# A hybrid decoder layer on one core: attention in pairs of query blocks, input halves scaled one by one, and precedence for softmax and chain

## The chip, the cores and the metric

The kernel runs on one core of a Trainium2 chip. The time is device microseconds (us) of one execution. Each figure is the median of several executions unless it says that it is one profiled execution. The engines are TensorE (PE in the profile; PEld is its weight load), VectorE (DVE), ScalarE (ACT), GpSimd (POOL) and SyncE (SP), which issues the DMAs.

## The reference

The kernel computes one layer of a decoder with 1024 tokens and 1024 columns in float32:

```python
h = rmsnorm(x)                       # one combined input projection follows
# mixer A, 4 heads of 128: gated DeltaNet on q, k, v with a causal convolution of width 4,
#   S_t = a_t (I - b_t k_t k_t^T) S_{t-1} + b_t k_t v_t^T ;  o_t = S_t^T q_t
#   (in chunks: a triangular solve, then a chain of states), times silu(z)
# mixer B, 8 heads of 64: dilated sliding-window attention,
#   (window, dilation) in (128,1), (512,4), (2048,16), the branches merged
#   by their softmax denominators
x = x + concat(A, B) @ wo            # one output projection
gate, up = halves of causal_dwconv(rmsnorm(x) @ w_up)    # width 3
x = x + (silu(gate) * up) @ w_down                       # MLP of width 2816
out = rmsnorm(x)
```

The lines are shortened. Products of 128x128 weights with 512 tokens are written out as three products of high and low parts (`mm3`: xhi with whi, xlo with whi, xhi with wlo), so that the reduced-precision matmul mode gives nearly float32 results. Such a matmul is called a dense matmul below. Smaller products run in plain float32 as two or four passes.

## The kernel before, in words

The layer is one program in which many pieces of work are interleaved on TensorE.

*The planner.* `Weave` (lines 42 to 114) holds generator functions with levels: `norms` 0, `gates` 1, the preparation of keys 3, of queries and values 4, the chain 1, `attention` 5, `out_proj` 8, `dense` 9, the MLP 8. Each yields the time it has still to wait, by a model of each engine; `Weave.run` continues the ready one with the lowest level. The result is TensorE's written order. The other engines' orders come from the scheduler of the tile framework, which takes instructions by readiness and by their place in the program. Each engine then runs its own list strictly in order. All helper instructions of VectorE, ScalarE, GpSimd and SyncE are recorded at line 132, matmuls at line 177 and transposes at line 181.

*The stages in time.* From 0 to 107 us the first dense products and the preparation of keys run. From 107 to 229 the query and value columns run, with forward substitution and the merging of the inverse blocks in between. From 229 to 304 the four chains run: at each of 8 chunks of 128 tokens a state passes from TensorE to VectorE and ScalarE and back (`chain`, lines 733 to 797). From 313 to 493 attention runs, mixed with the dense products of the attention columns and of the gates z. Dense products and the output projection end at about 615; then come the second norm, the MLP's upper part (to 1028) and its lower part (to 1258). The MLP and its weights are not touched by the change.

*Dense columns.* `dense` (line 462) takes 25 columns of 128 one after the other (`first`, line 319, has done three columns of keys). A column has two halves of 512 tokens; each half is 24 dense matmuls into one bank of the `hf` ring. `scaled` then multiplies a half by the tokens' reciprocal norms (`rstdB`) on VectorE into a tile of 1024 (`xr`; `aqkv` for attention's columns, in the order of residue classes, which `apark` stores in DRAM). Key columns do that for each half when its bank is done; all others for both at the end of the column. `conv_silu` and `silu2` then work on the tile.

*Attention.* There are 4 pairs of heads (the two heads `e` of a pair lie in the two halves of the partitions) and 8 query blocks of 128 tokens for each, so 32 items. For an item, `scores` multiplies queries with up to 256 near keys and with keys of the same residue class, into two banks of tag `asc`; VectorE adds the mask and takes the extreme (`tensor_tensor_reduce`, in the profile CUSTOM_DVE_ANT), ScalarE takes the exponential with its sum, VectorE the reciprocal, and ScalarE multiplies by it. `turn` transposes the result through banks of tag `atr`: VectorE copies the near part to `pt` and ScalarE the far part to `pb`. `values` multiplies `pt` with the values into the bank `po`, and after four items `merge_classes` adds the far products and `give` copies `po` out to `oT`. `advance` orders it: scores of an item, values of the item two before, transposes of the item one before. `att_values` transposes the values of the next pair of heads between the last block of one and the first block of the next.

*Output projection.* `mixer_splits` loads each head's output `ot` (or takes `og` or `oT`), and splits it into `ohi` (ScalarE) and `olo` (VectorE). `out_proj` (line 1003) takes heads k = 0 to 7 in order, for two groups of output columns at once, once the last group of attention has begun.

Of the kernel before, what the change touches and what calls it, by code (L numbers as in the profile page):

```python
# [35 lines left out]
MSLACK = 1.5  # L36
MGAP = 0.6
# [79 lines left out]
class Engine:  # L117


    def __init__(self, wv, eng, name, fixed, per, lag=0.28):  # L120
        self.args = wv, eng, name, fixed, per, lag

    def __getattr__(self, op):
        wv, eng, name, fixed, per, lag = self.args

        def call(*a, **kw):
            aps = [x for x in a + tuple(kw.values()) if hasattr(x, "tensor")]
            acc = [kw["accum_out"]] if "accum_out" in kw else []
            n = float(np.prod(aps[0].shape[1:]))
            us = 0.3 + 0.165 * n if kw.get("op") == OP.pow else fixed + per * n  # L130
            wv.account(name, us, aps[:1] + acc, aps[1:], lag)
            return getattr(eng, op)(*a, **kw)  # L132
        return call


def hybrid_layer(tc, I, out):
# [3 lines left out]
    ac = Engine(wv, nc.scalar, "scalar", 0.12, 0.00085)  # L140
    po_ = Engine(wv, nc.gpsimd, "gpsimd", 0.15, 0.0021)
# [163 lines left out]
    wba = tile_(sp, [P, KT, 32], F32, "wba", "t1", 3)  # L305
# [117 lines left out]
    def conv_silu(pair, j, name, tag):  # L423
        xr = scaled(pair, "xr") if isinstance(pair, list) else pair
# [16 lines left out]
    def silu2(pair, name):  # L441
        xr = scaled(pair, "xr")
# [19 lines left out]
    def dense():  # L462
# [5 lines left out]
        for i, col in enumerate(DENSE):  # L468
# [7 lines left out]
            for hh in range(2):  # L476
                pt = bank("hf")
                yield wv.need(pt, *w)
                for k in range(KT):
                    mm3(pt, [t[:, k, :] for t in w], [t[:, half(hh)] for t in xs[k]], k == 0, k == KT - 1)  # L480
                    yield 0.0
                pair.append(pt)
                if kind == "k":
                    if hh == 0:
                        xr = A("xr", "go")
                    scaled(pair, "xr", t=xr, hs=(hh,))
# [3 lines left out]
            elif kind == "q":  # L490
                q = conv_silu(pair, h, "qT", "qa")
                wv.add(4, qprep(h, q))
            elif kind == "v":
                v = conv_silu(pair, 8 + h, "vT", "qa")
                wv.add(4, vprep(h, v))
            elif kind == "z":
                og = gated[h] = A("og", "kT*")
                sy.dma_start(og, mixer[h])
                ve.tensor_tensor(og, og, silu2(pair, "zz"), op=OP.mult)
            else:  # L500
                sy.dma_start(apark[h, col[2]], scaled(pair, "aqkv", True))
# [109 lines left out]
    def forward_sub():  # L611
# [6 lines left out]
        tmp = tile_(sp, [P, 256], F32, "tmp", "t1", 3)  # L618
# [111 lines left out]
    def chain(h):  # L730
# [14 lines left out]
        for c in range(NCH):  # L745
# [12 lines left out]
            else:  # L758
# [3 lines left out]
                ve.scalar_tensor_tensor(r, ps[:, 0:P], ngam[:, c, h:h + 1], vtok[:, cs], op0=OP.mult, op1=OP.add)  # L762
# [3 lines left out]
            if c < NCH - 1:  # L766
                wke = tile_(sp, [P, P], F32, "wke", "r" + tg, 1)
                ve.tensor_scalar(wke, ps[:, P:2 * P], ke[:, c:c + 1], None, op0=OP.mult)
            ac.activation(w, ps[:, P:2 * P], AF.Copy)
            if c < NCH - 1:  # L770
# [3 lines left out]
                if c == 0:  # L774
                    ve.tensor_copy(sn, ps[:, 2 * P:3 * P])
                else:
                    ve.scalar_tensor_tensor(sn, st, ge[:, c:c + 1], ps[:, 2 * P:3 * P], op0=OP.mult, op1=OP.add)
# [6 lines left out]
            ac.activation(vtok[:, cs], po[:, :P], AF.Copy, scale=rq[:, c:c + 1])  # L784
            if c:
                ve.scalar_tensor_tensor(vtok[:, cs], po[:, P:2 * P], gq[:, c:c + 1], vtok[:, cs], op0=OP.mult,
# [4 lines left out]
            ac.activation(osq, vtok[:, cs], AF.Square, accum_out=ms[:, c:c + 1])  # L791
# [30 lines left out]
    def att_values(vT):  # L822

        vn, vc = A("vn", "kt"), A("vc", "kt")
        for hh in range(2):
# [4 lines left out]
            ac.activation(vn[:, half(hh)], pt, AF.Copy)  # L830
        for c in range(4):
# [7 lines left out]
    def attention():  # L839
        for h in range(H):  # L840
            yield from wv.until(("o", h))
        mks = [A("mk", "go") for _ in range(2)]
        sy.dma_start(mks[0], I["mk"][0])
        sy.dma_start(mks[1], I["mk"][1])
        yield from wv.until(("a", 0, 2))
# [10 lines left out]
        def scores(it):  # L856
            n, q, k, nb = it["n"], it["q"], it["k"], it["nb"]
            pss = [bank("asc") for _ in range(2)]
            yield wv.need(*pss, q, k)
            k0 = max(n - 1, 0) * P  # L860
            n1_, n2_ = (n + 1) * P - k0, P * nb
            wd = n1_ + n2_
            for e, er in enumerate(HALVES):
                mm(pss[e][:, :n1_], q[er, n * P:(n + 1) * P], k[er, k0:k0 + n1_], 0.0009 * n1_)
            for c in range(4):
                o = slice(32 * c, 32 * c + 32)
                for e, er in enumerate(HALVES):
                    mm(pss[e][o, n1_:wd].rearrange("p (n u) -> p n u", u=32), q[er, n * P + 32 * c:n * P + 32 * c + 32],
                       by_block(k)[er, :4 * nb, c, :], 0.00025 * n2_, tile_position=(64 * e, 32 * c))
            sm = A("sm", "dv*", shape=(P, 2, 512))  # L870
            mx = tile_(sp, [P, 4], F32, "mx", "mx", 4)
            mn, den = mx[:, :2], mx[:, 2:]
            mv, m = mask(n)
            for e in range(2):
                ve.tensor_tensor_reduce(out=sm[:, e, :wd].rearrange("p (a b) -> p a b", a=m),
                                        in0=pss[e][:, :wd].rearrange("p (a b) -> p a b", a=m), in1=mv, scale=-0.125,
                                        scalar=-NEG, op0=OP.add, op1=OP.min, accum_out=mn[:, e:e + 1])
            for e in range(2):
                ac.activation(sm[:, e, :wd], sm[:, e, :wd], AF.Exp, bias=mn[:, e:e + 1], scale=-1.0,
                              accum_out=den[:, e:e + 1])  # L880

            ve.reciprocal(den, den)
            for e in range(2):
                ac.activation(sm[:, e, :wd], sm[:, e, :wd], AF.Copy, scale=den[:, e:e + 1])
            it.update(sm=sm, wd=wd, n1=n1_, k0=k0)

        def turn(it):
            sm, wd, n1_ = it["sm"], it["wd"], it["n1"]
            it["pt"] = []
            for e in range(2):  # L890
                pt = tile_(sp, [P, 256], F32, "pt", "t1", 3)
                it["pt"].append(pt)
                pp = bank("atr")
                yield wv.need(pp, sm)
                for i in range(wd // P):
                    tp(pp[:, i * P:(i + 1) * P], sm[:, e, i * P:(i + 1) * P])
                ve.tensor_copy(pt[:, :n1_], pp[:, :n1_])
                ac.activation(it["pb"][e][:, it["u"]].rearrange("p b t -> p (b t)"), pp[:, n1_:wd], AF.Copy)

        def values(it):  # L900
            u = it["u"]
            yield wv.need(it["po"], *it["pt"])
            for i in range(it["n1"] // P):
                for e, er in enumerate(HALVES):
                    mm(it["po"][er, u * P:(u + 1) * P], v8(it["vn"])[:, it["k0"] // P + i, er],
                       it["pt"][e][:, i * P:(i + 1) * P], 0.12, u == 0 and i == 0, False, skip_group_check=True)

        def merge_classes(g):
            vcv = g["vc"].rearrange("p (c b d) -> p c b d", c=4, b=2)
            po, nb = g["po"], g["nb"]  # L910
            yield wv.need(*g["pb"])
# [23 lines left out]
        def advance(it):  # L935
            if it is not None:
                yield from scores(it)
            pipe.insert(0, it)
            if len(pipe) > 2:
                done = pipe.pop()  # L940
                if done is not None:
                    yield from values(done)
                    if done["u"] == 3:
                        yield from merge_classes(done["g"])
                        give(done["g"])
            if len(pipe) > 1 and pipe[1] is not None:
                yield from turn(pipe[1])

        for pi in range(4):
            q, k, vn, vc = cur  # L950
            for hh in range(2):
# [9 lines left out]
                for u in range(4):  # L961
                    yield from advance(dict(n=4 * hh + u, u=u, q=q, k=k, vn=vn, nb=nb, po=po, pb=pb, g=g))
            if pi < 3:
                cur = qkv[:2] + (yield from att_values(qkv[2]))
        for _ in range(2):
            yield from advance(None)
# [36 lines left out]
    def out_proj():  # L1003
# [4 lines left out]
        pts = {m: [bank(t) for _ in range(2)] for m, t in zip(MORDER, ("hf", "ch"))}  # L1008
        for k in range(8):
            yield from wv.until(("ot", k))  # L1010
            for m, w in zip(MORDER, ws):
                for h in range(2):
                    yield wv.need(pts[m][h], *w, *ots[k])
                    mm3(pts[m][h], [t[:, k, :] for t in w], [t[:, half(h)] for t in ots[k]], k == 0, k == 7)
# [471 lines left out]
```

## Time and profile before

| | us |
|---|---|
| median of three runs | 1258.36 |
| lowest, highest | 1257.86, 1259.85 |
| the profiled execution | 1259.56 |
| its span | 1257.8 |
| TensorE busy in it | 1233.0 |

In the profile a row of a group names the line, engine, operation, output and input tiles, shapes and count, and then, behind the bars, the busy time in us with the mean of one in ns, and the idle time of the engine just before them with what ended it. A row of the timeline begins with the start and the duration in us. A row of waits says who waited for whom: total us, times, and the longest. A matmul's duration overlaps with its neighbours', so what one costs is read from start to start.

### The profile page before, as it was taken

How to read it: one execution, taken by the hardware profiler on the slowest of the kernel's cores; microseconds unless marked ns; L12 is line 12 of the kernel's file. 1: busy time of each engine (PE TensorE's matmuls, PEld its weight loads, DVE VectorE, ACT ScalarE, POOL GpSimd, SP SyncE). 2: the span in 40 equal slices, each digit the busy share in tenths (PEclk: the TensorE clock that was granted, in tenths of full speed). 3: DMA queues.
4: the chain of work that ended last, by engine and by line, in shares of the span. 5: the costliest groups of instructions: out<-in, count | busy, mean ns of one | idle time of the engine just before them, and what ended most of it. 6: DMA issues, size and time to landing. Idle time of an engine off the chain costs nothing.

```text
span 1257.8 us, 18320 instructions
## 1 busy us (share of the span) xinstructions
PE 1233.0 (98%) x7040; PEld 1002.1 (80%) x7040; DVE 936.0 (74%) x1462; ACT 621.8 (49%) x1179; POOL 47.8 (4%) x34
## 2 busy tenths in 40 slices
PE   9989999999999999999999999999999999999996
PEld 7768887888676767878788888888888888787886
DVE  7566975563555455676798888888988989899875
ACT  7374444462757374465554454544544454343451
POOL 0021110022000000000000000000000000000000
PEclk9989999999999999999999999999999999999998
DMA  6313244255223420454312313223223298545523
GB/s 228 100 57 94 85 116 137 101 160 206 96 78 100 140 63 26 126 179 139 118 51 101 92 59 101 85 67 101 79 73 101 68 353 290 167 138 198 192 85 134
DMA packets 81974, 153.52 MB, mean 122 GB/s; under 512 B 21824, under 2 KB 32736, under 8 KB 81888
## 3 DMA queue, kind: packets, MB, share of 16 engines
q1 hardware_dynamic: 81888, 152.37, 37.1%
q8 instruction: 55, 0.90, 0.3%
q14 instruction: 31, 0.25, 0.1%
HBM read 114.31 MB, written 35.93 MB: 119 GB/s over the span
## 4 chain that ended last, share of the span: by engine, by line
PE 84%; DVE 7%; DMA 4%; ACT 2%; issue 2%; SPq 0%; POOL 0%; POOLq 0%; DVEq 0%; ACTq 0%
PE ps L177 44%; PE pa L177 18%; PE pc L177 9%; PE dw L177 8%; PE ps L181 4%; DMA wd<-in_wd 3%; DVE pr L132 2%; DVE x1h L132 1%; DVE wd L132 1%; ACT dec L132 1%; DVE kT L132 1%; PE warm L177 1%; DMA wst<-in_wu 0%; DVE r L132 0%; DVE xr L132 0%
## 5 line engine op out<-in xcount | busy, mean ns | idle before, releaser
L177 PE MATMUL dw<-pr 128*128 128x512 f32 (+1 forms) x984 | 213.3, 377 | 2.8 <-DVE x1h L132 2.8
L177 PEld LDWEIGHTS dw<-pr 128*128 128x128 f32 x984 | 176.1, 188 | 38.9 <-DVE x1h L132 4.9
L177 PE MATMUL ps<-xhi,whi 128*128 128x512 f32 x448 | 186.5, 416 | 0.0
L177 PE MATMUL ps<-xhi,wlo 128*128 128x512 f32 x448 | 175.8, 392 | 0.0
L177 PE MATMUL ps<-xlo,whi 128*128 128x512 f32 x448 | 175.3, 391 | 0.0
L177 PE MATMUL pa<-T,pair 128*128 128x512 f32 x528 | 127.1, 389 | 0.6 <-ACT u L132 0.6
L177 PEld LDWEIGHTS pa<-T,pair 128*128 128x128 f32 x528 | 99.0, 188 | 21.1 <-ACT u L132 0.7
L177 PEld LDWEIGHTS ps<-xhi,whi 128*128 128x128 f32 x448 | 84.6, 189 | 19.9 <-issue 6.0
L177 PEld LDWEIGHTS ps<-xhi,wlo 128*128 128x128 f32 x448 | 84.4, 188 | 18.5
L177 PEld LDWEIGHTS ps<-xlo,whi 128*128 128x128 f32 x448 | 84.8, 189 | 13.5
L132 ACT ACTIVATE sm<-sm,mx 128x512 f32<-128x512 f32 (+2 forms) x128 | 79.9, 651 | 23.0 <-DVE mx L132 23.0
L132 ACT ACTIVATE u<-pa 128x512 f32<-128x512 f32 x44 | 26.4, 600 | 110.5 <-PE pa L177 110.5
L132 DVE SCALAR_TENSOR_TENSOR y<-xu,fcw,y 128x1023 f32<-128x1023 f32 (+1 forms) x44 | 56.3, 1281 | 25.7 <-ACT y L132 25.7
L132 ACT ACTIVATE whi<-wst 128x1024 fp32r<-128x1024 f32 (+2 forms) x38 | 38.7, 1017 | 70.4 <-PE ps L177 63.0
L177 PE MATMUL pc<-B,pair 128*128 128x512 f32 x264 | 63.4, 389 | 0.0
L177 PE MATMUL pa<-B,A 128*128 128x512 f32 x264 | 63.4, 389 | 0.0
L177 PE MATMUL pc<-T,S 128*128 128x512 f32 x264 | 63.4, 389 | 0.0
L177 PE MATMUL pa<-T,S 128*128 128x512 f32 x264 | 63.4, 389 | 0.0
L132 ACT ACTIVATE pr<-wd 128x1024 fp32r<-128x1024 f32 x33 | 35.0, 1061 | 55.0 <-DVE wd L132 36.5
L132 DVE TENSOR_TENSOR wst<-wst 128x512 f32<-128x512 f32 x88 | 60.5, 687 | 0.7
L177 PE MATMUL ps<-B,pair 128*128 128x512 f32 x252 | 60.5, 389 | 0.0
L177 PEld LDWEIGHTS pc<-B,pair 128*128 128x128 f32 x264 | 49.6, 188 | 10.3
(230 smaller groups left out, 2279.8 us busy)
## 6 DMA issues: line engine op xcount, KB each, us to landing
wst<-in_wu SPq DMA_DIRECT2D x44, 512.0 KB, 3.7
wd<-in_wd SPq DMA_DIRECT2D x44, 512.0 KB, 4.3
wst<-in_wi SPq DMA_DIRECT2D x25, 512.0 KB, 3.7
upark<-y SPq DMA_DIRECT2D x22, 512.0 KB, 3.7
apark<-aqkv SPq DMA_DIRECT2D x12, 512.0 KB, 2.8
r<-upark SPq DMA_DIRECT2D x11, 512.0 KB, 7.6
r<-upark SPq DMA_DIRECT2D x22, 256.0 KB, 6.7
wa<-in_wd SPq DMA_DIRECT2D x22, 256.0 KB, 2.9
```

Source lines behind the costliest of these rows:

```text
L132: return getattr(eng, op)(*a, **kw)
L177: tc.stamp_issue_order_token(nc.tensor.matmul(dst, lhs, rhs, start=start, stop=stop, **kw).ins, TOKEN)
L181: tc.stamp_issue_order_token(nc.tensor.transpose(dst, src, ident).ins, TOKEN)
```

## The change

The change has these parts.

1. `Engine` gets an argument `first`. With it, an instruction is issued under the scheduler's high priority (`offset=400`). The new wrappers `uv` (VectorE) and `ua` (ScalarE) are used in the chain and in attention's softmax and evacuations.
2. Each half of every dense column is scaled when its bank is done. `conv_silu` and `silu2` take the scaled tile.
3. Attention takes query blocks in pairs. The scores of both blocks use four banks (two `asc`, two `atr`); the multiplication by the reciprocal is on VectorE; the four groups of transposes alternate between the two tags; `pt` is one tile for a pair, from the ring `dv*`. `advance` orders: transposes of the last pair, scores of this pair, values of the last pair. The next pair of heads' values are transposed between the transposes and the scores at the last step of a pair of heads.
4. The masks are loaded after the last chunks of two chains instead of after all heads' outputs. The wait for the outputs itself stays.
5. `out_proj` takes whichever head is ready, the first of the two column groups ahead, and the second only when attention is finished.
6. The planner's costs in attention change, and it gets slacks of its own for transposes and values (`TSLACK`, `PSLACK`). A load of the re-ordered values `vc` is entered as ready 6.0 us later.

```diff
 class Engine:
-            return getattr(eng, op)(*a, **kw)
+            if first is None:
+                return getattr(eng, op)(*a, **kw)
+            with first(offset=URGENT):
+                return getattr(eng, op)(*a, **kw)
...
+    uv = Engine(wv, nc.vector, "vector", 0.07, 0.00105, first=tc.high_priority)
+    ua = Engine(wv, nc.scalar, "scalar", 0.12, 0.00085, first=tc.high_priority)
...
 # dense
-                if kind == "k":
-                    if hh == 0:
-                        xr = A("xr", "go")
-                    scaled(pair, "xr", t=xr, hs=(hh,))
+                if hh == 0:
+                    xr = A("aqkv" if kind == "a" else "xr", "go" if kind == "k" else "ev")
+                scaled(pair, "xr", kind == "a", t=xr, hs=(hh,))
...
 # chain (r, wke, the state, vtok: ve to uv; w, vtok, osq: ac to ua)
-                ve.scalar_tensor_tensor(r, ps[:, 0:P], ngam[:, c, h:h + 1], vtok[:, cs], op0=OP.mult, op1=OP.add)
+                uv.scalar_tensor_tensor(r, ps[:, 0:P], ngam[:, c, h:h + 1], vtok[:, cs], op0=OP.mult, op1=OP.add)
...
+        wv.ready[vc.tensor.name] = max(wv.pe, wv.ready[vn.tensor.name]) + 6.0
+        wv.free["sync"] = max(wv.pe, queue) + 1.6
...
-        for h in range(H):
-            yield from wv.until(("o", h))
+        for h in range(2):
+            yield from wv.until(("c", h, NCH - 1))
         mks = [A("mk", "go") for _ in range(2)]
         sy.dma_start(mks[0], I["mk"][0])
         sy.dma_start(mks[1], I["mk"][1])
+        for h in range(H):
+            yield from wv.until(("o", h))
...
-            for e in range(2):
-                ac.activation(sm[:, e, :wd], sm[:, e, :wd], AF.Copy, scale=den[:, e:e + 1])
+                uv.tensor_scalar(sm[:, e, :wd], sm[:, e, :wd], den[:, e:e + 1], None, op0=OP.mult)
...
+        def turn(pair):
+            pts = A("pt", "dv*", shape=(P, 4, 256))
+            for b, (it, tag) in enumerate(zip(pair, ("asc", "atr"))):
+                sm, wd, n1_ = it["sm"], it["wd"], it["n1"]
+                it["pt"] = []
+                for e in range(2):
+                    pt = pts[:, 2 * b + e, :]
+                    it["pt"].append(pt)
+                    pp = bank(tag)
+                    yield wv.need(pp, sm, slack=TSLACK[b])
+                    for i in range(wd // P):
+                        tp(pp[:, i * P:(i + 1) * P], sm[:, e, i * P:(i + 1) * P])
+                    turned(it, e, pt, pp)
...
+        def advance(pair, more=None):
+            done = pipe.pop() if pipe else None
+            if done is not None:
+                yield from turn(done)
+            if more is not None:
+                last["values"] = yield from more
+            if pair is not None:
+                yield from scores(pair)
+                pipe.append(pair)
+            if done is not None:
+                yield from values(done)
+                if done[1]["u"] == 3:
+                    yield from merge_classes(done[0]["g"])
+                    give(done[0]["g"])
...
 # out_proj
-        for k in range(8):
-            yield from wv.until(("ot", k))
-            for m, w in zip(MORDER, ws):
+        todo = [(k, j) for k in range(8) for j in range(2)]
+        while todo:
+            now = [a for a in todo if ("ot", a[0]) in wv.done and (a[1] == 0 or "attention" in wv.done)]
+            if not now:
+                yield 0.3
+                continue
+            k, j = now[0]
+            todo.remove(now[0])
```

More of the change, by code (lines that the diff above doesn't have):

```diff
@@ L439, in conv_silu, with silu2 @@
         return y
-    def silu2(pair, name):
-        xr = scaled(pair, "xr")
+    def silu2(xr, name):
         y = A(name, "ev")
@@ L498, in dense @@
                 sy.dma_start(og, mixer[h])
-                ve.tensor_tensor(og, og, silu2(pair, "zz"), op=OP.mult)
+                ve.tensor_tensor(og, og, silu2(xr, "zz"), op=OP.mult)
             else:
-                sy.dma_start(apark[h, col[2]], scaled(pair, "aqkv", True))
+                sy.dma_start(apark[h, col[2]], xr)
                 wv.done.add(col)
@@ L830, in att_values @@
             ac.activation(vn[:, half(hh)], pt, AF.Copy)
+        queue = wv.free["sync"]
         for c in range(4):
@@ L908, in merge_classes, with values @@
+        def values(pair):
+            yield wv.need(pair[0]["po"], *pair[0]["pt"], slack=-PSLACK)
+            for it in pair:
+                u = it["u"]
+                for i in range(it["n1"] // P):
+                    for e, er in enumerate(HALVES):
+                        mm(it["po"][er, u * P:(u + 1) * P], v8(it["vn"])[:, it["k0"] // P + i, er],
+                           it["pt"][e][:, i * P:(i + 1) * P], 0.11, u == 0 and i == 0, False, skip_group_check=True)
         def merge_classes(g):
@@ L960, in attention @@
                 g = dict(po=po, pb=pb, nb=nb, hh=hh, pi=pi, vc=vc)
-                for u in range(4):
-                    yield from advance(dict(n=4 * hh + u, u=u, q=q, k=k, vn=vn, nb=nb, po=po, pb=pb, g=g))
+                for u in (0, 2):
+                    more = att_values(qkv[2]) if (hh, u) == (1, 2) and pi < 3 else None
+                    yield from advance([dict(n=4 * hh + i, u=i, q=q, k=k, vn=vn, nb=nb, po=po, pb=pb, g=g)
+                                        for i in (u, u + 1)], more)
             if pi < 3:
-                cur = qkv[:2] + (yield from att_values(qkv[2]))
-        for _ in range(2):
-            yield from advance(None)
+                cur = qkv[:2] + last["values"]
+        yield from advance(None)
+        wv.done.add("attention")
     ots = {}
```

129 lines of the change are left out of this document (58 added, 71 removed).

## The prediction

> **What bounds the kernel now.** I read the engine totals first, then the busy time stage by stage, then the chain of waits, and last the timeline of a typical attention step. The engine totals and the slices of the page:
>
> ```profile
> PE 1233.0 (98%) x7040; PEld 1002.1 (80%) x7040; DVE 936.0 (74%) x1462; ACT 621.8 (49%) x1179; POOL 47.8 (4%) x34
> PE   9989999999999999999999999999999999999996
> DVE  7566975563555455676798888888988989899875
> ```
>
> TensorE (PE) is busy for 1233.0 of 1257.8 us. A change can gain only by making TensorE's own work shorter or by taking some of the 25 us in which it stands. The stages, in the columns from:to, PE, PEld, DVE, ACT, POOL, clock, DMA:
>
> ```profile
> 66.00:70.00 4.00, 0.93 (x5) 0.43 (x3) 4.00 (x6) 4.00 (x13) 0.00 (x0) 1.00 0.40 131
> 70.00:74.00 4.00, 2.65 (x10) 2.53 (x11) 2.34 (x3) 3.97 (x16) 1.40 (x1) 0.53 0.01 4
> 74.00:78.00 4.00, 4.00 (x17) 3.40 (x16) 4.00 (x9) 4.00 (x13) 2.26 (x1) 0.62 0.00 0
> 200.00:276.00 76.00, 74.80 (x641) 65.22 (x640) 46.97 (x125) 38.91 (x144) 8.02 (x5) 1.00 0.37 123
> 276.00:300.00 24.00, 23.46 (x134) 19.86 (x133) 8.85 (x23) 10.06 (x30) 7.23 (x5) 1.00 0.63 213
> 313.24:493.04 179.80, 179.34 (x1668) 128.00 (x1668) 93.47 (x254) 111.71 (x273) 0.00 (x0) 1.00 0.27 87
> 516.00:616.00 100.00, 99.12 (x438) 81.15 (x436) 71.31 (x103) 53.20 (x83) 0.00 (x0) 1.00 0.46 156
> 623.00:1028.00 405.00, 405.00 (x1789) 335.42 (x1788) 356.14 (x402) 193.52 (x253) 0.00 (x0) 1.00 0.30 96
> ```
>
> Attention (313 to 493, mixed with dense products) leaves TensorE 0.46 us idle; the MLP, none. The idle time lies early (66 to 74, in the key preparation), in the chains (1.2 + 0.5 us in 200 to 300), and behind attention (0.9). The chain of waits shows what a dense matmul costs when nothing is late:
>
> ```profile
> 631.21 2.72 PE pa L177 x12
> ```
>
> That is 2.72/12 = 0.2265 us from start to start. The timeline of one attention step gives the cost of changing from one kind of matmul to another (columns: start, duration, engine, operation):
>
> ```profile
> 340.18 0.66 PE L177 MATMUL ps<-pt,vn 128*64 128x128 f32 x8
> 340.77 1.24 PE L181 MATMUL ps<-ident,sm 128*128 128x128 f32 x8
> 341.76 0.47 PE L177 MATMUL ps<-xhi,whi 128*128 128x512 f32 x1
> 342.63 1.29 PE L177 MATMUL ps<-kT,qT 64*128 64x256 f32 x20
> 343.86 0.66 PE L177 MATMUL ps<-pt,vn 128*64 128x128 f32 x8
> 344.44 0.50 PE L177 MATMUL ps<-xhi,whi 128*128 128x512 f32 x1
> 347.31 1.03 PE L181 MATMUL ps<-ident,sm 128*128 128x128 f32 x8
> 348.10 0.47 PE L177 MATMUL ps<-xhi,whi 128*128 128x512 f32 x1
> ```
>
> Start to start: eight transposes right behind values take 341.76 - 340.77 = 0.99; between dense pieces they take 348.10 - 347.31 = 0.79. Three dense matmuls ahead of scores take 0.87 where 3 x 0.2265 = 0.68; twelve from 344.44 take 2.87 where 2.72 is due. So a change of kind costs 0.15 to 0.20 us.
>
> **The change, part by part.**
>
> *Pairs in attention.* The number of matmuls is the same in both kernels. The orders differ: before, each of 32 blocks has its own scores, values and transposes; now 16 pairs have them, and each group of eight transposes stands between dense pieces. Removed are 16 entries into values, 16 into scores (the second block's follow the first's), and about 21 cases of transposes next to values or scores: 53 changes x 0.20 = -10.6 us. At 0.15 each it is -8.0; at 0.10 (should the pairs make new changes) -5.3. I take -10.6, since the 0.99 against 0.79 is like for like.
>
> *What the pairs then wait for.* The rows that price the softmax (VectorE, then ScalarE):
>
> ```profile
> L132 DVE CUSTOM_DVE_ANT_1 sm<-ps,mk 128x512 f32<-128x512 f32 x24 | 15.6, 689 | 7.7 <-PE ps L177 7.7
> L132 DVE DVE_READ_ACCUMULATOR2_ANT mx<- 128x1 f32 x64 | 5.4, 84 | 0.0
> L132 DVE RECIPROCAL mx<-mx 128x2 f32<-128x2 f32 x32 | 5.2, 161 | 11.8 <-ACT sm L132 11.7
> L132 DVE TENSOR_TENSOR xr<-ps,rstdB 128x512 f32<-128x512 f32 x32 | 21.8, 689 | 21.4 <-PE ps L177 21.0
> L132 DVE COPY pt<-ps 128x256 f32<-128x256 f32 x56 | 22.4, 419 | 10.7 <-PE ps L181 10.2
> L132 DVE TENSOR_TENSOR olo<-og,ohi 128x1024 fp32r<-128x1024 f32 x4 | 4.7, 1222 | 2.0 <-ACT ohi L132 2.0
> L132 DVE TENSOR_TENSOR olo<-ot,ohi 128x512 fp32r<-128x512 f32 x7 | 4.8, 692 | 4.0 <-ACT ohi L132 3.9
> L132 DVE TENSOR_SCALAR um<-ps 64x512 f32<-64x512 f32 x2 | 1.4, 682 | 1.4 <-PE ps L177 1.3
> L132 DVE TENSOR_SCALAR ssk<-ssk 128x8 f32<-128x8 f32 x4 | 0.7, 170 | 9.4 <-ACT sq L132 9.4
> L132 ACT ACTIVATE sm<-sm,mx 128x512 f32<-128x512 f32 x64 | 44.3, 718 | 12.0 <-DVE mx L132 12.0
> L132 ACT ACTIVATION_READ_ACCUMULATOR sm<-sm,mx 128x1 f32 x64 | 12.1, 188 | 0.0
> L132 ACT ACTIVATE ohi<-og 128x1024 fp32r<-128x1024 f32 x4 | 4.0, 1054 | 6.8 <-PE ps L177 4.1 <-DVE og L132 2.7
> L132 ACT ACTIVATE pb<-ps 128x256 f32<-128x256 f32 x32 | 11.5, 381 | 8.0 <-DVE pt L132 7.9
> ```
>
> The normalisation leaves ScalarE for VectorE, as a tensor_scalar of up to 512 elements, on-chip memory to on-chip memory. No row shows that: the 8-element form takes 0.17, the 512-element one from PSUM 0.68. I take the middle, 0.42. The Trainium skill, page "VectorE: DVE Perf Modes", section "Mode 2×_2P", says that an fp32 tensor_scalar between SBUF operands reaches two results per cycle while tensor_tensor doesn't; from the page's cycle counts I estimate 0.42 for 512. At 0.68 every pair's softmax would be about 1 us longer on VectorE. At 0.42, 64 of them add at most 27 us to VectorE's 93.47 of 179.80: it does not become full. In most pairs 15 to 18 dense matmuls (3.4 to 4.1 us) stand between the values and the transposes, and hide the softmax. Three pairs are not quite covered, since pt copies stand behind 1.2 us instructions of VectorE: 0.65 + 0.70 + 0.45 = +1.8 us, between 0 and half a 1.22 instruction for each of 16 pairs (+9.8).
>
> *The end of attention.* The planner's new order uses up the dense work earlier. Before, 531 dense matmuls stand behind the last attention piece (99 of the z columns, 432 of out_proj). Now out_proj gives 12 between the last pieces and 420 after them. The last four pieces are thinly covered:
>
> - Scores of the last pair stand right behind the transposes of pair 14 and need all four banks. In ScalarE's order two ohi stand behind that pair's exponentials, in VectorE's two olo stand before the pt copies. The last pt copy ends 2 x 1.054 + 1.222 + 4 x 0.419 + 0.69 (an xr) = 5.7 us behind the last exponential; TensorE is ready after about 2.2 (reciprocal 0.16, two normalisations 0.84, eight transposes 0.99, a change of kind 0.2). Stall 3.5.
> - The last softmax: four reductions of 0.689 + 0.084 = 3.1, of which 0.6 lie under the second block's scores; then olo 1.22, olo 0.69, reciprocal 0.16, olo 0.69 and two normalisations 0.84, in VectorE's order: 6.1 from the last score. The cover is values 0.59 and six dense 1.36. Stall 4.1.
> - Behind that: bank for the second transposes 0.5, last values 1.5, classes 0.6 (pb behind ohi), oT 0.5 (its bank): 3.1. The six dense between the transposes hide the rest; were they gone, +1.4.
>
> Together +10.7. Lower end: the olo and ohi are done early and only the bare softmax stays, 2.5 + 0.16 + 0.84 - 1.95 = 1.6, with 1.0 behind it: +2.6. Upper end: as above with every copy behind one more olo (4 x 0.69): +13.5.
>
> *Third query preparation.* Its scores' products now follow its eight transposes directly; before, 15 dense (3.4 us) stood between. They wait for ScalarE's evacuations:
>
> ```profile
> L132 ACT ACTIVATE sq<-ps 128x128 f32<-128x128 f32 x64 | 17.6, 275 | 4.8 <-PE ps L181 3.5
> L132 ACT ACTIVATION_READ_ACCUMULATOR sq<-ps 128x1 f32 x64 | 12.6, 198 | 0.0
> L132 ACT ACTIVATE vT<-xr,gcw 128x1024 f32<-128x1024 f32 x4 | 4.6, 1150 | 0.0
> PE ps L177 <- ACT sq L132: 5.0, 2, 4.4
> ```
>
> In ScalarE's order one vT of 1.15 stands among the eight sq of 0.47 each. The first four products wait for four sq and the vT, 3.0, less the second four transposes, half of 0.79: 2.6. The last four, with dense work between, I put at 0.7. Stall 3.3. The first preparation is closer too: +0.3. Together +3.6, from 0 to 5.0. The last row is the same wait in the key preparation before, 5.0 in two.
>
> *Precedence (uv, ua).* Ready chain and softmax instructions move ahead of dense evacuations. Of the chains' 1.7 us of idle time I take -1.2. At best -1.7; at worst +1, if a dense bank is freed a 0.69 later.
>
> *Halves.* Each half is scaled when its bank is done, 12 x 0.2265 = 2.7 us or more earlier. TensorE has other dense work meanwhile: 0. Its cover is the second bank; gone, it would cost one 0.69 at a column. The tile is held longer, by 24 matmuls or 5.4 us; no column waits for that buffer in my reading of the order.
>
> *Mask loads, sync, out_proj.* SyncE's queue has the same loads in nearly the same order; the masks come two chains earlier and nothing in attention is behind them: 0. out_proj takes ready heads first: its start stalls before, 0.5 of the 0.9 idle in 516 to 616, go: -0.5. Fewer changes of kind at 107 to 229: -0.3.
>
> Sum: -10.6 + 1.8 + 10.7 + 3.6 - 1.2 - 0.5 - 0.3 = +3.5 us. The profiled execution took 1259.56 (span 1257.8); the median is 1258.36, 1.2 lower. Forecast: 1258.4 + 3.5, rounded down for the end's wide lower side (2.6 against 10.7), **1261.0**. Its own range, with the end between 6 and 13.5: 1257 to 1265.
>
> **Rivals.**
>
> *The saved changes win.* The olo and ohi at the end run ahead of the last softmax, because their inputs are there earlier than I think, and the end costs 2.6 instead of 10.7, the third preparation nothing: -10.6 + 1.8 + 2.6 + 0.3 - 2.0 = -7.9, that is 1250.5; half-way, 1254. For it: TensorE idles 0.46 us in the whole stage before, so the old order left nothing waiting. Against it: the order on each engine is fixed, and olo stands between reductions and reciprocal. It decides once all new stalls stay under 12.6 - 2.5 = 10. Chance 0.30.
>
> *The clock falls.* In 66 to 70 TensorE worked 0.93 of 4 us, and in 70 to 78 its granted clock was 0.53 and 0.62: (0.47 + 0.38) x 4 = 3.4 us lost. Stalls of 3.5 and 4.1 could each do the same at the end: 1261 + 3.4 = 1264.4, or 1267.8 for both. The Trainium skill, page "TensorE: Matmul & The Clock Gate", section "What's actually happening", has the clock halved after one idle window of about 3.4 us, free-running; the rows agree with that, and by it my stalls are just at the edge. Against it: both stalls are broken by pieces of work. Chance 0.15.
>
> *VectorE's order starves each pair.* Half a 1.22 instruction late in 16 pairs, +9.8 in place of 1.8: 1269. For it: VectorE's slices rise to 8 and 9 near the end of attention. Chance 0.12.
>
> *Nothing comes of it.* The gains are 8.0 (0.15 each) and the end 6: within 0.2%, 1258.4. Chance 0.10.
>
> **How the numbers follow.** 0.2% is 2.5 us, about what a measurement of this kernel can tell from no change. My forecast has 0.33, of which 0.18 is above 1260.9 and 0.12 within, 0.03 below. Faster: 0.27 of the first rival and 0.03: 0.30. Same: 0.12 + 0.03 + 0.10 = 0.25. Slower: 0.18 + 0.15 + 0.12 = 0.45. The range 1251 to 1268 takes in the first rival nearly to its end and the clock; VectorE's rival and the tails are left out.
>
> **What would show it.** Right: attention's transposes take 0.79 in nearly all groups; TensorE's waits show pt, pb or sm as releasers within 20 us of the last score, some 8 to 12 us in all; a wait of ScalarE's sq before the third query's products. Wrong: idle time at the end under 4 us, tensor_scalar near 0.68 or 0.2, clock under 1.00 behind attention, or waits for mx and pt in each pair.

## The result, and the profile after

| | median, us | ratio to before, 95% interval |
|---|---|---|
| before | 1258.12 | |
| after | 1253.72 (1252.73 to 1256.28) | 0.9965 (0.9953 to 0.9976) |

The change is 4.4 us faster; the forecast was 1261.0, slower. The profiled execution took 1253.64 us with a span of 1251.9.

The page of the kernel after, its engine totals:

```profile
PE 1224.5 (98%) x7040; PEld 1009.5 (81%) x7040; DVE 957.2 (76%) x1526; ACT 585.1 (47%) x1115; POOL 45.1 (4%) x34
```

TensorE has the same 7040 records and 8.5 us less busy time. With the 64 normalisations ScalarE gave up 36.7 us, and VectorE took on 21.2.

To see where the time went I divided each trace at four points: the first 32x32 product (the end of the preparation), the first transposes of values for attention, the last class product, and the second norm. From each stretch I subtract its dense matmuls at 0.2265 us, because the orders move dense work between stretches. What is left is the time of everything else, waits and changes of kind included. For attention the lengths are 179.80 us with 348 dense matmuls before and, by the second row of the next fence, 200.21 us with 462 after.

| us beside dense work | before | after | difference | forecast |
|---|---|---|---|---|
| preparation, to 189 (before) and 197 (after) | 47.53 | 52.25 | +4.7 | +3.3 |
| substitution and chains | 61.66 | 59.66 | -2.0 | -1.2 |
| attention | 100.98 | 95.57 | -5.4 | +1.9 |
| output projection | 2.01 | 1.84 | -0.2 | -0.5 |
| second norm and MLP | 31.63 | 28.90 | -2.7 | 0 |

Attention is the row with the wrong sign. (The last row belongs to no part of the change, see below.) The preparation's +4.7 is the forecast wait of the third query, and a clock that fell behind it (0.57 in the first row further down). TensorE's wait of after, from its list for 107 to 320 us; before has none for `sq` there:

```profile
PE ps L186 <- ACT sq L136: 2.4, 1, 2.4
```

The busy time by stage after, in the columns used before; the last three are the granted clock, DMA share and GB/s:

```profile
180.00:184.00 4.00, 4.00 (x19) 3.63 (x18) 3.44 (x9) 1.62 (x6) 1.64 (x1) 0.57 0.43 68
315.28:515.49 200.21, 196.44 (x1783) 155.02 (x1782) 138.22 (x344) 90.02 (x226) 0.00 (x0) 0.98 0.32 103
495.00:500.00 5.00, 3.53 (x21) 2.50 (x19) 4.86 (x8) 3.15 (x6) 0.00 (x0) 1.00 0.32 107
500.00:505.00 5.00, 5.00 (x55) 3.54 (x54) 4.97 (x11) 2.83 (x5) 0.00 (x0) 0.66 0.78 256
505.00:510.00 5.00, 2.70 (x12) 2.30 (x11) 4.31 (x11) 3.73 (x10) 0.00 (x0) 0.77 0.44 161
510.00:515.00 5.00, 5.00 (x53) 4.27 (x54) 3.56 (x8) 2.71 (x6) 0.00 (x0) 0.89 0.16 58
```

The clock was 1.00 in all of attention before. Now it falls to 0.66, 0.77 and 0.89 in the last 15 us, which is (0.34 + 0.23 + 0.11) x 5 = 3.4 us of TensorE's work lost. The timeline of that end on TensorE (start, duration, operation, and idle time before it with its releaser):

```profile
495.83 1.03 PE L190 MATMUL ps<-ident,sm 128*128 128x128 f32 x8
496.79 0.92 PE L186 MATMUL ps<-kT,qT 64*128 64x256 f32 x4
499.18 2.13 PE L186 MATMUL ps<-kT,qT 64*128 64x256 f32 x36 [1.47 <-ACT pb L138]
501.24 1.97 PE L186 MATMUL ps<-pt,vn 128*64 128x128 f32 x16
507.63 1.86 PE L190 MATMUL ps<-ident,sm 128*128 128x128 f32 x8 [2.30 <-DVE sm L138]
```

and on VectorE and ScalarE:

```profile
493.53 2.35 DVE L136 TENSOR_TENSOR olo<-og,ohi 128x1024 fp32r<-128x1024 f32 x2
495.80 0.75 DVE L138 COPY pt<-ps 128x256 f32<-128x256 f32 x2
497.06 0.74 DVE L138 COPY pt<-ps 128x256 f32<-128x256 f32 x2
501.48 0.68 DVE L138 CUSTOM_DVE_ANT_1 sm<-ps,mk 128x512 f32<-128x512 f32 x1
503.92 1.22 DVE L136 TENSOR_TENSOR olo<-og,ohi 128x1024 fp32r<-128x1024 f32 x1
505.06 0.68 DVE L136 TENSOR_TENSOR olo<-ot,ohi 128x512 fp32r<-128x512 f32 x1
507.01 0.88 DVE L138 TENSOR_SCALAR sm<-sm,mx 128x512 f32<-128x512 f32 x2
496.86 1.05 ACT L136 ACTIVATE whi<-wst 128x1024 fp32r<-128x1024 f32 x1
497.81 1.05 ACT L136 ACTIVATE zz<-xr 128x1024 f32<-128x1024 f32 x1
498.76 0.65 ACT L138 ACTIVATE pb<-ps 128x256 f32<-128x256 f32 x2
```

Both forecast stalls are there, and their recorded idle times, 1.47 and 2.30, are smaller than the forecast 3.5 and 4.1. The last scores wait for the far copies `pb`, which stand behind `whi` and `zz` on ScalarE. The two `olo` that the forecast put in their way ran from 493.5 to 495.9. They did keep the first two `pt` copies back, but TensorE had six dense matmuls and the second transposes to do meanwhile. The last softmax is as long as forecast, with `olo` in its order (from the last score at 501.2 to the first transposes at 507.6, 6.4 against 6.1), but its cover, slowed by the clock, lasts 4.1 instead of 1.95.

From the transposes at 495.83 to the end of the class products at about 515.7 it is 19.9 us. The same pieces at their usual durations (transposes 0.79 to 0.97, scores 2.08, values 0.92, twelve dense 3.0, classes 1.9) make 11.6. So the end cost 8.3: 3.4 of clock and 4.9 of stalls, of which the record shows 3.8 as idle time.

These two parts are not independent. The first fall of the clock slowed work that only covered the wait for the last softmax. In the kernel without precedence (number 4 below), which has TensorE's order of the change, the clock stayed at 1.00 from 490 to 505 us and fell once, behind the wait, to 0.66 over 505 to 510. TensorE's waits for that softmax in the change, and in kernel 4:

```profile
PE ps L190 <- DVE sm L138: 2.3, 1, 2.3
PE ps L190 <- DVE sm L136: 3.9, 1, 3.9
```

What the clock did not take, the wait took: attention beside dense work is 95.6 and 95.4. So the softmax stall by itself is about the forecast 4.1, and one fall of 0.34 x 5 = 1.7 us, not two, made the end longer.

The rest of attention saved 5.4 + 8.3 = 13.7 us. In that rest TensorE's list of waits (315 to 495 us) is empty. One pair's scores after, and the values behind them:

```profile
486.04 2.16 PE L186 MATMUL ps<-kT,qT 64*128 64x256 f32 x40
488.12 1.09 PE L186 MATMUL ps<-pt,vn 128*64 128x128 f32 x16
```

Two blocks' scores take 488.12 - 486.04 = 2.08; before, one block's took 343.86 - 342.63 = 1.23, two 2.46. That is 0.38 a pair, 6 us for 16, where the forecast had 16 changes x 0.20 = 3.2.

### The profile page after: what moved, and what is told of

Its sections match the earlier page's. It is cut to its first block, busy times and chain, and to the rows that moved or that the text cites. A ratio compares the mean times of both kernels' runs of the same rounds, so it can differ in the third digit from the quotient of the medians.

```text
span 1251.9 us, 18318 instructions
## 1 busy us (share of the span) xinstructions
PE 1224.5 (98%) x7040; PEld 1009.5 (81%) x7040; DVE 957.2 (76%) x1526; ACT 585.1 (47%) x1115; POOL 45.1 (4%) x34
## 4 chain that ended last, share of the span: by engine, by line
PE 83%; DVE 7%; DMA 5%; ACT 2%; issue 2%; POOL 0%; SPq 0%; POOLq 0%; DVEq 0%; ACTq 0%
PE ps L186 44%; PE pa L186 18%; PE pc L186 9%; PE dw L186 8%; PE ps L190 3%; DMA wd<-in_wd 3%; DVE pr L136 2%; DMA r<-upark 1%; DVE x1h L136 1%; DVE wd L136 1%; ACT dec L136 1%; DVE kT L136 1%; PE warm L186 1%; DMA wst<-in_wu 0%; DMA ot<-mixer 0%
## 5 line engine op out<-in xcount | busy, mean ns | idle before, releaser
L136 DVE SCALAR_TENSOR_TENSOR y<-xu,fcw,y 128x1023 f32<-128x1023 f32 (+1 forms) x44 | 56.4, 1281 | 25.7 <-ACT y L136 25.6
L138 ACT ACTIVATE sm<-sm,mx 128x512 f32<-128x512 f32 (+2 forms) x64 | 41.2, 645 | 42.3 <-DVE mx L138 42.3
L186 PEld LDWEIGHTS pa<-B,A 128*128 128x128 f32 x264 | 49.6, 188 | 10.3
L186 PEld LDWEIGHTS pa<-T,S 128*128 128x128 f32 x264 | 49.6, 188 | 10.3
```

The source lines that it names most:

```text
L186: tc.stamp_issue_order_token(nc.tensor.matmul(dst, lhs, rhs, start=start, stop=stop, **kw).ins, TOKEN)
```

## The experiments

All ratios are to the kernel before, timed beside it on the same chip.

| | median, us | ratio, 95% interval | preparation | chains | attention |
|---|---|---|---|---|---|
| before | 1258.1 to 1259.4 | | 47.5 | 61.7 | 101.0 |
| after | 1253.72 | 0.9965 (0.9953 to 0.9976) | 52.3 | 59.7 | 95.6 |
| 1 no halves | 1252.17 | 0.9948 (0.9935 to 0.9960) | 48.1 | 61.4 | 94.6 |
| 2 pairs only | 1252.41 | 0.9946 (0.9933 to 0.9960) | 47.8 | 62.2 | 94.6 |
| 3 query spaced | 1257.16 | 0.9985 (0.9973 to 0.9997) | 49.1 | 62.8 | 96.0 |
| 4 no precedence | 1254.80 | 0.9962 (0.9947 to 0.9977) | 50.2 | 59.7 | 95.4 |
| 5 near, far by block | 1254.90 | 0.9963 (0.9948 to 0.9977) | 50.4 | 59.7 | 95.1 |
| 6 no pairs | 1262.51 | 1.0026 (1.0015 to 1.0038) | 52.3 | 59.8 | 102.2 |
| 7 ScalarE normalises | 1252.81 | 0.9944 (0.9929 to 0.9960) | 52.4 | 59.7 | 92.6 |
| 8 the same, no halves | 1251.50 | 0.9937 (0.9922 to 0.9951) | 47.6 | 62.3 | 94.4 |
| 9 halves only | 1263.01 | 1.0029 (1.0018 to 1.0041) | 50.3 | 59.7 | 104.6 |
| 10 q, v whole | 1253.51 | 0.9954 (0.9942 to 0.9967) | 47.9 | 60.2 | 96.3 |
| 11 the same, end covered | 1247.19 | 0.9913 (0.9899 to 0.9926) | 47.9 | 60.2 | 90.8 |
| 12 q, v whole, ScalarE normalises | 1249.36 | 0.9922 (0.9909 to 0.9934) | 47.8 | 60.1 | 92.6 |

The last three columns are us beside dense work in the profiled execution, divided as above.

**1 and 2: which part gains.**

```diff
 # 1: the kernel after, with the dense loop of before
-                if hh == 0:
-                    xr = A("aqkv" if kind == "a" else "xr", "go" if kind == "k" else "ev")
-                scaled(pair, "xr", kind == "a", t=xr, hs=(hh,))
+                if kind == "k":
+                    if hh == 0:
+                        xr = A("xr", "go")
+                    scaled(pair, "xr", t=xr, hs=(hh,))
...
-                q = conv_silu(xr, h, "qT", "qa")
+                q = conv_silu(pair, h, "qT", "qa")
```

> The change without its second part: the halves of a dense column are scaled together at the column's end, as before; pairs, precedence and the rest stay. In the compiled order 15 dense matmuls stand again between the third query's transposes and its products, and 15 instead of 6 cover the last softmax. Theory A (the pairs save more than forecast, and the halves only move dense work away from where it is needed): the query's 4 us and half of the end's 8 us come back, 1253.7 - 8 = 1246, and the granted clock stays near 1.00 behind attention. Rival B (the halves free banks earlier and are part of the gain): 1255 or more.

> The kernel before with attention in pairs alone (with its planner's costs and early mask loads; normalisation on VectorE); halves, precedence and the output projection's choice are left as before. Theory A: the pairs are the whole gain, 13 us of changes of kind less some 4 us left at the end, 1258.1 - 9 = 1249, and 1 to 3 us above the run without halves, by what precedence is worth. Rival B: pairs need precedence, waits for pt and sm in each pair, 1254 or more.

Kernel 2 is the kernel before with the function `attention` of the change (on plain engines), `att_values`, and the slacks. Both are at least as fast as the change (the intervals just overlap), so theory A holds in sign: the pairs are the gain, and rival B falls twice, for halves and for precedence. The sizes were too hopeful (1252.2 and 1252.4, where 1246 and 1249 were expected). In both the granted clock stayed 1.00 at the end of attention, as expected, but attention beside dense work fell only 1.0 below the change's. The reason is new waits, most of them not at the end: three for the softmax, between 378 and 427 us, and one of 0.8 for a `pt` copy at the end. TensorE's waits of kernel 1, 315 to 510 us:

```profile
PE ps L190 <- DVE sm L138: 4.7, 3, 2.4
PE ps L186 <- DVE pt L138: 0.8, 1, 0.8
```

Kernel 2 has the same two waits. Without halves the planner's order covers the end and uncovers the middle. Kernel 2 also has the early mask loads and the planner's new costs, which belong to the function `attention`; no run takes them apart from the pairs.

**3: the third query's wait by itself.** One line of the planner:

```diff
-                yield wv.need(pt, *w)
+                yield wv.need(pt, *w, slack=-6.0 if (i, hh) == (9, 0) else 0.0)
```

> The changed kernel with one slack changed in the planner, so that 9 dense matmuls stand between the third query's transposes and its products (none in the change); everything else keeps its order. Theory A: the wait for ScalarE's squares goes (2.6 + 1.2 us in the trace), 1253.7 - 3.5 = 1250. Rival: that dense work is itself late (its weights), so that the wait only moves: 1253 to 1254.

The wait for the squares went (preparation 52.3 to 49.1), and the next stretch became 3.1 longer. TensorE's list of waits of this kernel, 185 to 318 us, and its clock in part of that time:

```profile
PE ps L186 <- issue: 1.5, 1, 1.5
PE ps L186 <- ACT w L138: 0.7, 2, 0.5
```

```profile
192.00:230.00 38.00, 36.52 (x516) 28.45 (x515) 19.27 (x28) 14.13 (x35) 1.64 (x1) 0.96 0.38 128
```

The row "issue" is new; it is time for which the profile shows no releaser, and its cause stays open. The other half is the clock: it fell behind that gap, and 0.04 x 38 is 1.5 us. So the gain went in the next stretch, as the rival has it, but that the dense work's own lateness is the reason is not shown. The time, 1257.16, lies above both expectations. Of the 2.7 us by which this profiled execution (1256.33) is longer than the change's, 2.1 lie in the MLP, whose order is the same.

**4: precedence.**

```diff
-    uv = Engine(wv, nc.vector, "vector", 0.07, 0.00105, first=tc.high_priority)
-    ua = Engine(wv, nc.scalar, "scalar", 0.12, 0.00085, first=tc.high_priority)
+    uv = Engine(wv, nc.vector, "vector", 0.07, 0.00105)
+    ua = Engine(wv, nc.scalar, "scalar", 0.12, 0.00085)
```

> The changed kernel with plain VectorE and ScalarE instructions in chain and softmax (no high priority); TensorE's order is the same. Theory A: precedence is worth about the 2 us that the chains' stage lost, and some at the pairs: 1255 to 1257. Rival C: precedence is what keeps the pairs free of waits, each of 16 pairs is half a microsecond late without it: 1262 or more. Rival D: it does nothing: 1253.7.

The chains take 59.7 and attention 95.4, as in the change, and the ratios are 0.9962 and 0.9965. That is rival D. (The preparation is 2.0 shorter by the clock alone, see the last section.) The 2 us that the chains' stretch lost are not precedence; kernel 9 shows whose they are.

**5: the entries into the scores.** The loop over near scores and the loop over far scores become one:

```diff
-            for it in pair:
-                n, n1_, wd = it["n"], it["n1"], it["wd"]
+                wd = it["wd"]
                 for c in range(4):
```

> The changed kernel with the scores of a pair written block by block (near, far, near, far) in place of near, near, far, far. It only puts back 16 entries into the far scores and 16 into the near ones that the pairs had joined. Theory A (the forecast counted one entry per block where there are two; each costs 0.19): attention's scores take 32 x 0.19 = 6 us less in the change than before, half of it by this order: 3 us more here, 1256.7; TensorE's scores in attention go from 29 to 32 us. Rival: the saving lies in the banks and waits, not in the entries: the same time, 1253.7.

One pair's scores in this kernel:

```profile
496.07 2.52 PE L186 MATMUL ps<-kT,qT 64*128 64x256 f32 x40
498.52 1.09 PE L186 MATMUL ps<-pt,vn 128*64 128x128 f32 x16
```

They take 2.45 in place of 2.08. Over attention all scores, start to start, sum to 34.9 us, before to 35.4, and in the change to 29.2 without the stall in the last. So joining near with near and far with far is worth 5.7 us. It does not show in the time (1254.9), for the planner's order with it leaves 18 dense matmuls over the last softmax instead of 6: the end's stalls shrink, and attention as a whole is 0.5 shorter beside its dense work (95.6 to 95.1) although the scores are 5.7 longer. The size that I expected here, 3, was half of what the order carries, and the time is the rival's: it was right for another reason than its own.

**6 and 9: what the rest does without pairs.** Kernel 6 is the change with attention of before; kernel 9 is before with the change's `dense`, `conv_silu` and `silu2`.

> The changed kernel with attention of the kernel before (one block at a time, normalisation on ScalarE); precedence in the chain, halves and the output projection's choice stay. Theory A: the pairs are the whole gain; the 13.7 us of changes of kind come back, the 8 us at the end go (507 dense matmuls stand behind attention), the query's wait of 2.6 stays: 1253.7 + 5.5 = 1259, the same as the kernel before or 1 slower. Rival: the other parts bring 2 us or more: 1256.

> The kernel before with its dense columns scaled half by half, nothing else changed. In the compiled order this alone takes the 15 dense matmuls from between the third query's transposes and its products. Theory A: it is slower by that wait, 2.6 us, and by 2 more where the granted clock falls after it: 1260.5 to 1263. Rival: earlier scaling frees banks, and the time is that of the kernel before or less.

Both are slower than before by the same 0.3%: 1262.5, where 1259 was expected, and 1263.0. Halves alone give all of kernel 6's loss, so precedence and the output projection's choice are worth nothing that can be measured. (The early mask loads are in neither kernel.) Halves alone also give the 59.7 in the chains' stretch. What they lose by: the query's wait, and in attention of before a new wait. In kernel 9's profiled execution the granted clock fell behind that wait too, to 0.66 over 320 to 330 us; in kernel 6's it did not, which may be why their attention differs (104.6 and 102.2). The two longest rows of TensorE's waits of kernel 9, 170 to 500 us:

```profile
PE ps L177 <- ACT sq L132: 2.4, 1, 2.4
PE ps L177 <- DVE mx L132: 1.8, 1, 1.8
```

**7 and 8: the normalisation back on ScalarE.**

```diff
-                uv.tensor_scalar(sm[:, e, :wd], sm[:, e, :wd], den[:, e:e + 1], None, op0=OP.mult)
+                ua.activation(sm[:, e, :wd], sm[:, e, :wd], AF.Copy, scale=den[:, e:e + 1])
```

> The changed kernel with the normalisation back on ScalarE (718 ns for 512 elements instead of 482 on VectorE). In the compiled order 459 dense matmuls stand behind attention in place of 420, and 18 instead of 6 cover the last softmax. Theory A: the longer softmax is covered by more dense work in each pair, and the end's stalls shrink by 4: 1250. Rival: ScalarE's longer chain shows in each pair, 16 x 0.3 = 5: 1258.

> The same as the one before, and the halves of a column scaled together at its end. Theory A: the query's wait goes too (2.6 to 4.6): 1247 to 1250, the fastest of all. Rival: the halves' part and the end's are one and the same, no faster than the run without halves: 1252.

VectorE's normalisation is the shorter instruction, by this row after against ScalarE's 718 before:

```profile
L138 DVE TENSOR_SCALAR sm<-sm,mx 128x512 f32<-128x512 f32 x32 | 14.1, 482 | 0.5
```

The kernels with the longer one are not slower, 0.9944 and 0.9937. The planner gives each pair's softmax other cover, and 459 and 441 dense matmuls stand behind attention instead of 420. Theory A holds in direction only for 7 (1252.8, not 1250, and the intervals overlap); for 8 the gain over kernel 1 is 0.7 us, which the intervals do not separate, and that is the rival.

**10, 11 and 12: keep the halves where they do no harm.**

```diff
-                if hh == 0:
+                if hh == (1 if kind in ("q", "v") else 0):
                     xr = A("aqkv" if kind == "a" else "xr", "go" if kind == "k" else "ev")
-                scaled(pair, "xr", kind == "a", t=xr, hs=(hh,))
+                if kind not in ("q", "v"):
+                    scaled(pair, "xr", kind == "a", t=xr, hs=(hh,))
+                elif hh == 1:
+                    scaled(pair, "xr", t=xr)
 # 11 besides
-TSLACK = -0.6, -0.4
+TSLACK = -0.8, -0.6
```

> The changed kernel with the query and value columns alone scaled at the column's end; attention's and z's columns keep their halves. Attention's order is that of the change, 18 dense matmuls stand between the third query's transposes and its products. Theory A: 2.6 to 4.6 us go and nothing else: 1250 to 1251. Rival (as the run with the wait spaced out): the wait moves to the forward substitution: 1253 or more.

> The one before, and the planner's slack for the transposes from -0.6, -0.4 to -0.8, -0.6, so that each pair uses less dense work and 12 dense matmuls stand ahead of the last scores (none in the change) and 18 behind the last values (6). Theory A: the end's 8 us shrink to 2, and the granted clock stays 1.00 there: 1245 to 1247. Rival: each pair, thinner covered, waits for its softmax, and the sum is the same: 1250.

> The run with whole query and value columns, and the normalisation on ScalarE. Attention's order is that of the run with the normalisation on ScalarE. Theory A: its attention (92.6 us beside the dense work) and the kernel before's preparation (47.6) together: 1252.8 - 4.6 = 1248. Rival: 1251, like the run with all halves undone.

Kernel 10 loses the query's wait (47.9), but gives 0.5 back in the chains and 0.7 in attention; in the profiled executions another 1.4 lie in the MLP. Its time is not distinguishable from the change's. That is the rival's number, but not its cause: only 0.5 of the wait shows up in the next stretch. Kernel 11 differs from it by 0.2 us of slack and is the fastest, 1247.19. It uses 450 dense matmuls in attention instead of 462 and keeps 12 ahead of the last scores and 18 behind the last values. Two stages of its end, and its waits (311 to 510 us):

```profile
490.00:495.00 5.00, 5.00 (x65) 3.35 (x64) 4.26 (x9) 2.85 (x5) 0.00 (x0) 1.00 0.35 100
500.00:505.00 5.00, 4.18 (x51) 3.40 (x52) 4.87 (x7) 2.46 (x6) 0.00 (x0) 1.00 0.65 213
```

```profile
PE ps L190 <- DVE sm L138: 1.4, 1, 1.4
PE ps L186 <- DVE pt L138: 1.1, 2, 0.8
```

The clock is 1.00 again and attention takes 90.8 in place of 96.3 in kernel 10: 5.4 us for the end's cover. That kernel beats before by 0.87% and the change by 0.5% (0.9913/0.9965). Kernel 12 covers the end by the other way, 0.9922; its 1249.36 lies between theory and rival.

## Why the prediction was wrong

The forecast was 1261.0 and 1253.72 was measured, 7.3 us less. Attention alone accounts for that much: +1.9 forecast, -5.4 measured in the profiled execution. The step that failed most is "53 changes x 0.20 = -10.6"; the two other terms of attention, +1.8 and +10.7, were too high by 1.8 and 2.4.

- *Changes of kind: right mechanism, count too low.* The step took one entry per block's scores. There are two, into the near and into the far ones, so a pair had four, and two of them go when it runs near, near, far, far. Scores lost 6.2 us (35.4 to 29.2) instead of 3.2; transposes lost 4.4 (25.7 to 21.3) and values 2.8 (17.5 to 14.7), near the forecast. (The groups that the end disturbed are counted at their usual length.) Kernel 5 shows the missing term. The measured sum, by the stage's length, is 13.7.
- *Waits in each pair, +1.8: none.* This term came from instructions of 1.2 us standing ahead of a `pt` copy in VectorE's order. They do stand there: the two copies at 495.80 (row above) begin 1.2 us behind the end of the first transposes, and one at 461.26 begins 1.4 late behind a `zz`. But TensorE has dense work or scores over them, and its list of waits from 315 to 495 us is empty. The step that was wrong is the overlap. (The rival on VectorE leaned on slices of 8 and 9 near the end of attention. That was misread: attention's slices before are 5, 5, 5, 4, 5, 5, and the 8 and 9 begin at 629 us, in the MLP.)
- *End of attention, +10.7: 8.3.* The term had three stalls. The last softmax, 4.1, was right in place, cause and size, as kernel 4's 3.9 shows. The stall of the last scores is there, but by `whi` and `zz` on ScalarE and not by `olo`, and from start to start it cost 4.45 - 2.08 = 2.4 instead of 3.5. The third, 3.1 behind the softmax, is not there. In its place came about 1.7 of clock. The recorded idle time, 3.8, is under the 4 that the prediction named as a sign of being wrong, but only because the slower clock stretched the cover: kernel 4 records 5.4.
- *The rival "the saved changes win"* gave 1254 as its half-way value, which is what was measured. That is luck: it had the end at 2.6 and no wait of the third query, and its saving was the same -10.6.
- *The clock* was held as a rival at 0.15 and came with the stalls. The four profiled kernels with this end (after, 3, 4, 10) all show it, 0.89 to 0.94 over 490 to 520; kernels with more cover (1, 2, 5, 7, 8, 11, 12) show 1.00. The Trainium skill, page "TensorE: Matmul & The Clock Gate", section "What's actually happening", has the clock halved after an idle window of about 3.4 us that runs free of the kernel. Here falls came behind recorded gaps of 1.5 and 2.4 us, and behind the same gap in some executions only.
- *Third query, +3.6: 2.4 of wait, and 2 of clock in this execution.* The stall of 3.3 measured 2.4, and the clock was not in the term; that the sum came near is luck. The owner was missed: I put the halves at 0 and named the wait under "third query preparation", though it is the halves that cause it (kernel 9). Taken away by itself (kernel 3) it brings nothing.
- *Precedence, -1.2: 0.* The stretch lost 2.0, by the halves' other order (kernels 4 and 9).
- *Normalisation, 0.42: 0.48.* 482 ns for 512 elements and 350 for 256 in the trace give 0.52 ns an element, half of the 1.04 of a tensor_tensor (1222 for 1024 and 689 for 512). The Trainium skill, page "VectorE: DVE Perf Modes", section "Mode 2×_2P", has fp32 tensor_scalar at twice the rate of tensor_tensor; the trace agrees with the rate and not with the estimate of 0.42.
- *The MLP, 0: -2.7 in the trace.* TensorE, VectorE and ScalarE have the same order there in all fourteen kernels. Over the fourteen traces this stretch varies between 28.9 and 33.2 us, with waits for `x1h` between 1.3 and 3.2; it is no part of the change. The change's trace happens to combine the lowest such value with a fall of the clock in the preparation, so two rows of the first table are partly chance, with opposite signs.

By the steps with measured sizes: -13.7 + 8.3 + 4.7 - 2.0 - 0.2 = -2.9, and -2.7 in the MLP: -5.6 of the 5.9 us between the two profiled executions (1259.56 and 1253.64); the other 0.3 lie behind the last matmul.

## What to carry to other kernels

Where TensorE is the bound, count every change from one kind of matmul to another, about 0.19 us each here, and group by kind (all near, then all far) even inside one step. When a group of work is to be hidden under other work, see that the cover lasts to its end: the last two pairs cost 8 us of the 13.7 that all sixteen had saved, and 0.2 us of slack in the planner gave 5 back. A long instruction ahead of a copy is no stall of TensorE as long as TensorE has other work over it: copies here began up to 1.4 us late, and TensorE waited for none of them from 315 to 495 us. In the same way a slower clock over work that only bridges a wait cost next to nothing.

## What was not expected of the hardware

The same wait of 2.4 us for ScalarE's squares was followed by a granted clock of 0.57 over 180 to 184 us in the change (row above), and by 1.00 in the kernel without precedence:

```profile
180.00:184.00 4.00, 4.00 (x24) 3.32 (x23) 3.81 (x12) 1.44 (x4) 1.64 (x1) 1.00 0.43 68
```

Of the six profiled kernels with that wait (after, 4, 5, 6, 7, 9) three show the fall, three do not. It costs 2.0 us (preparation 52.3 to 52.4 against 50.2 to 50.4). It may be one reason why the times of the change spread over 3.5 us; that is not shown.
